# The end of routing in a hybrid block with a PEER feed-forward: six row products, the gathers' index tiles and the splits for the gates in another order

## The chip, the cores and the metric

One core of a Trainium2 chip runs the whole block. The metric is the time of one execution on the device in microseconds (us), the median of the runs. Engines are named as the profile names them: PE is TensorE (matmuls; PEld its weight loads), DVE is VectorE, ACT is ScalarE, POOL is GpSimd, SP issues most of the transfers. POOL also issues transfers of its own, and all of the gathers.

## The reference

A residual block on 512 tokens of width 1024, in float32: an RMS norm, a gated MLP group and a chunked attention group, an output projection, and then PEER, a feed-forward of 16384 single-neuron experts. The part that matters here is PEER:

```python
q = (xb @ w_query).reshape(PEER_TOKEN_BLOCK, PEER_HEADS, 2, PEER_HALF)
sc = jnp.einsum('thpd,hpkd->thpk', q, sub_keys).astype(jnp.float32)
s_top, i_top = lax.top_k(sc, PEER_TOPK)
...
best, pos = lax.top_k(cand, PEER_TOPK)
eidx = jnp.take_along_axis(cand_idx, pos, axis=-1)
g = jax.nn.softmax(best, axis=-1)
u = jnp.take(expert_u, eidx, axis=0)
h = jax.nn.gelu(jnp.einsum('thkd,td->thk', u, xb))
vv = jnp.take(expert_v, eidx, axis=0)
return jnp.einsum('thk,thkd->td', (g * h.astype(jnp.float32)).astype(xb.dtype), vv)
```

For each token and each of 8 heads, 16 experts are chosen (`eidx`) and weighted (`g`). The input row is multiplied with each chosen row of `expert_u`, and the results weight the rows of `expert_v`.

## The kernel before, in words

Two ways of computing PEER share the tokens. For most tokens the kernel multiplies densely: each of the 128 tiles of `expert_u` (512 KB each, `in_uT`) is loaded, split into a high and a low half (`hi` on ACT, L154; `lo` on DVE or POOL, L155) and multiplied on PE with the tokens' input in three products per step (`mm3`, L192 to L194, 8 steps a tile, 24 matmuls); an activation (L716) empties the result's PSUM bank, of which there are two, into `act`. The chosen weights are spread into a dense gate matrix, and a second product with the tiles of `expert_v` (L1168) ends the kernel. For the first 128 tokens, and for the last 64 (`UX`), the kernel gathers the chosen rows instead: an indirect transfer issued by POOL fetches one row of `expert_u` for each of 128 partitions (128 x 1024 float32), and DVE multiplies it with the input rows and sums it up (the "row product").

The last 64 tokens have 8 x 16 choices each, and two choices stand side by side on the 128 partitions, so there are 64 such gathers, 8 per head. They are the ones that the change touches:

- `indices_early(h)` brings one head's indices into `eui`: half of them by a small transfer on POOL's queue (L668), half by a cast on POOL (L669).
- `gather_early(n, ...)` issues the next n gathers (L653) into one of 6 row buffers (`ROWA`).
- `dots_early(lag)` multiplies gathered rows until only `lag` are left (L662, on DVE), into `du`.

The stages around them are these. Routing goes over the heads; in it PE interleaves query products with tiles of `expert_u`. Behind the last head come eight tiles of `expert_u` (`BRIDGE`) on PE, while DVE chooses that head's experts (L732 to L792), the softmax runs (L798 to L803), and the indices are taken apart into digits (`indices_of`, L866 to L871, into `ff`). Then two held tiles (`HELD`) are split on POOL, and routing ends. In routing a scheduler sets the order, by priorities and by marks (`tc.issue_after`).

The gate stage is a loop of 48 iterations (n) and two more, written out by hand for PE, DVE, ACT and POOL. PE turns `ff` (`gates_of`, L941), DVE makes digits from it (`hb`, `lb`, L952 and L955), POOL multiplies these to `bm` (L963), DVE makes `am` (L971), PE multiplies the two two iterations later (L979, 16 to an iteration), ACT copies the result out (L982, `gst`), and every second iteration stores 1 MB. Between these PE works on a few steps of the tiles of `expert_u`, which POOL or DVE split. `own` is 40; at n = `own` - 7 = 33 the row products of the last 64 tokens must be finished.

```python
if n < own - 7 and n % 3 < 2:
    gather_early(1, gat, ROWA)
dots_early(LAGE)
```

Of the kernel before, what the change touches and what calls it, by code (L numbers as in the profile page):

```python
# [11 lines left out]
I32 = mybir.dt.int32  # L12
# [7 lines left out]
P = 128  # L20
D = 1024
S = 512
TT = S // P
# [3 lines left out]
NH = 8  # L27
TOPK = 16
# [15 lines left out]
UX = 64  # L44
# [4 lines left out]
HS = NH * TOPK // 2  # L49
HK = TOPK // 2  # L50
# [9 lines left out]
ROWA = 6  # L60
LAGE = 3
BRIDGE = 8
EARLY = 6
# [29 lines left out]
def hybrid_block(tc, x, ln1, w_in, gng, wsT, bsb, qkg, bias, w_out, ln2, wq, skT, uT, ud, vd, out):  # L93
    nc = tc.nc
    ctx = ExitStack()
    with ctx:
# [10 lines left out]
        def pa():  # L107
            return ps_a.tile([P, 512], F32, name="pa", tag="pa")
# [13 lines left out]
        loads, splits, ready = [], [], []  # L122
        roots, behind_scale, behind_norm = [], [], []

        def queued_behind(marks):

            ctx = ExitStack()
            for i in marks:
                ctx.enter_context(tc.issue_after(i))
            return ctx  # L130
# [495 lines left out]
        eidx = rt.tile([P, TT, NH * TOPK], F32, name="eidx")  # L626
# [8 lines left out]
        gat = gat_ctx.enter_context(tc.tile_pool(name="gat", bufs=1, side="right"))  # L635
# [5 lines left out]
            nc.sync.dma_start(row[i * UX:(i + 1) * UX, :], xbd[1, P - UX:, :])  # L641
        nc.scalar.copy(xbu[:, 0:512], row[:, 0:512])
        nc.scalar.copy(xbu[:, 512:], row[:, 512:])
        eui = gat.tile([P, HS], I32, name="eui")
        du = gat.tile([P, HS], F32, name="du")
        dots = gat.tile([P, NH, 2, HK], F32, name="dots")
        early, issued = [], []

        def gather_early(n, rows_of, n_rows):

            for j in early[:n]:
                row = rows_of.tile([P, D], F32, name="rowe", tag="rowe", bufs=n_rows)
                nc.gpsimd.indirect_dma_start(out=row, out_offset=None, in_=ud,  # L653
                                             in_offset=bass.IndirectOffsetOnAxis(ap=eui[:, j:j + 1], axis=0))
                issued.append((j, row))
            del early[:n]

        def dots_early(lag):

            while len(issued) > lag:  # L660
                j, row = issued.pop(0)
                nc.vector.scalar_tensor_tensor(row, row, 1.0, xbu, op0=ALU.mult, op1=ALU.mult,  # L662
                                               accum_out=du[:, j:j + 1])

        def indices_early(h):

            js = slice(h * HK, (h + 1) * HK)
            nc.gpsimd.dma_start(eui[0:P - UX, js], eidx[P - UX:P, TT - 1, h * TOPK + HK:(h + 1) * TOPK])  # L668
            nc.gpsimd.tensor_copy(eui[P - UX:P, js], eidx[P - UX:P, TT - 1, h * TOPK:h * TOPK + HK])  # L669

        def ready_early(h):
            early.extend(range(h * HK, (h + 1) * HK))
# [38 lines left out]
        def multiply_tile(whole=False):  # L711
            multiply_some(KT, whole)
# [169 lines left out]
        for h in range(NH + 1):  # L882
            if h < NH:
                candidates(h)
            with queued_behind(found):
                dots_early(0)
            if h == NH:
                for i, _ in enumerate(first_products(sum(FILL) + BC, BRIDGE, nc.gpsimd, True)):
                    behind.append(done[0])
            if h > 1:  # L890
                with tc.issue_after(splits[0]):
                    indices_early(h - 2)
                    ready_early(h - 2)
                    gather_early(EARLY, gat, ROWA)
            if h > 0:
                hs = slice((h - 1) * TOPK, h * TOPK)
                ps = pa()
                mask = ps[:, 0:6 * ND * TOPK].bitcast(U32)
                powers = ps[:, 8 * ND * TOPK:8 * ND * TOPK + 6].bitcast(U32)
                nc.vector.tensor_copy(powers, bits)  # L900
                tree = rq.tile([P, ND, TOPK, 32], F32, name="tree", tag="tree", bufs=1)
                with tc.issue_after(behind[BRIDGE // 2 - 2]) if behind else ExitStack():
                    cand = pairs(rq, *top_pos.pop(h - 1)[:2], ND, ps[:, 6 * ND * TOPK:8 * ND * TOPK], True)
                with tc.issue_after(behind[BRIDGE // 2 - 1]) if behind else ExitStack():
                    choose(rq, cand, ND, gate[:, GT:, hs], eidx[:, GT:, hs], mask, tree,
                           nc.vector.tensor_copy if h >= NH - 1 else nc.scalar.copy, powers)
            if h == 4:

                with queued_behind(splits):
                    nc.gpsimd.tensor_copy(xch, xbh[:, :, T0:T0 + NDU])  # L910
                    nc.gpsimd.tensor_copy(xcl, xbl[:, :, T0:T0 + NDU])
# [10 lines left out]

        for _ in range(HELD):
            split_next()
        indices_early(NH - 1)
        ready_early(NH - 1)
        dots_early(0)
        routing.close()
        xn_ctx.close()

# [77 lines left out]
        engines = {getattr(mybir.EngineType, e) for e in ("PE", "DVE", "Activation", "Pool")}  # L1008
        own = steps - UX // TC
        with tc.manual_schedule(engines=engines):  # L1010
            gather_early(1, gat, ROWA)
            multiply_tile()
            gs[0] = gates_of(GT, ff.pop(0))
            dgs = {0: digits(gs[0], 0)}
# [2 lines left out]
            for n in range(steps + LEAD):  # L1017
# [11 lines left out]
                    activate_tile()  # L1029
                if n < steps:  # L1030
                    ams[n] = first_one_hot(gs[t], c)
                if n < own - 7 and n % 3 < 2:
                    gather_early(1, gat, ROWA)
                dots_early(LAGE)
                if t + 1 < ND:
                    if c == per - 5:
                        ff[t + 1] = indices_of(GT + t + 1)
# [210 lines left out]
```

## Time and profile before

| | |
|---|---|
| Median of three runs | 1442.33 us (1438.95 to 1442.57) |
| The profiled execution | 1436.48 us, of which 1434.4 us span |
| Granted TensorE clock, mean | 0.993 |
| End of routing, the last bridge tile to the first bm | 417 to 442 us |
| Gate stage | 442 to 592 us |
| Second product | 606 us to the end |

The span goes from the first to the last instruction. Starts in the trace are counted from its beginning. A row of the trace gives the start, the length, the engine, the line, the operation, what it writes and reads, and in brackets how long the engine stood idle before it and what it waited for. PE's matmuls are pipelined, so that a row's length is longer than the distance to the next row.

### The profile page before, as it was taken

Reading aid. Unit: us, or ns where it says so; the run is one execution under the profiler, and the core shown is the slowest. Engines: PE = TensorE matmul, PEld = TensorE weight load, DVE = VectorE, ACT = ScalarE, POOL = GpSimd, SP = SyncE. Lnnn points to the kernel's source line nnn. Section 1 sums busy time; section 2 is a strip of 40 time slices with the busy share of each in tenths; the row PEclk is TensorE's granted clock in tenths of the full one; section 3 lists DMA queues with packets and bytes.
Section 4 is the critical chain, followed back from the end, with each engine's and each line's share of the span. In section 5 each row is a group of like instructions: output and inputs, shape, how many; then the busy total and the mean of one; then the engine's idle time right before and its main releaser. Section 6 shows DMA issues by size and latency. Waiting matters only on the chain.

```text
span 1434.4 us, 21711 instructions
## 1 busy us (share of the span) xinstructions
PE 1391.9 (97%) x7838; PEld 1229.5 (86%) x7838; DVE 1150.5 (80%) x2502; ACT 611.4 (43%) x957; POOL 700.6 (49%) x487
## 2 busy tenths in 40 slices
PE   9999999999987978999999999999999999999998
PEld 7887788898986978898988898998998998888887
DVE  5537755998996888599999999889879888688883
ACT  5447635434442434554543444343333333333331
POOL 0002104678769988424554646545546455254520
PEclk9999999999998999999999999999999999999999
DMA  4352225667667998988998999999999989689981
GB/s 168 126 191 74 89 104 191 206 229 276 216 225 248 300 313 251 294 296 310 332 351 312 339 349 368 347 389 356 376 339 359 361 326 378 243 326 353 340 332 70
DMA packets 164330, 396.24 MB, mean 276 GB/s; under 512 B 12880, under 2 KB 75232, under 8 KB 162176
## 3 DMA queue, kind: packets, MB, share of 16 engines
q1 hardware_dynamic: 64640, 194.14, 37.6%
q0 software_dynamic: 48176, 173.46, 32.9%
q10 hardware_dynamic: 51408, 27.27, 6.6%
q8 instruction: 61, 1.00, 0.3%
q14 instruction: 45, 0.37, 0.1%
HBM read 363.34 MB, written 31.46 MB: 275 GB/s over the span
## 4 chain that ended last, share of the span: by engine, by line
PE 76%; DVE 9%; POOL 5%; DMA 4%; issue 3%; ACT 2%; another core or an unknown queue 0%; ACTq 0%; POOLq 0%; DVEq 0%; SPq 0%
PE pa L1168 22%; PE px L1168 11%; PE pu L194 9%; PE pu L192 9%; PE pu L193 9%; PE pa L192 4%; PE pa L979 3%; PE pa L193 3%; PE pa L194 3%; POOL bm L963 2%; POOL rowe L653 1%; DMA gd<-gst 1%; DVE lo L155 1%; POOL lo L155 1%; DVE row L1109 1%
## 5 line engine op out<-in xcount | busy, mean ns | idle before, releaser
L154 ACT ACTIVATE hi<-raw 128x1024 fp32r<-128x1024 f32 x296 | 312.8, 1058 | 468.5 <-DMA raw<-in_vd 124.0
L155 DVE TENSOR_TENSOR lo<-raw,hi 128x1024 fp32r<-128x1024 f32 x241 | 295.8, 1229 | 78.3 <-ACT hi L154 76.0
L1107 POOL DMA_INDIRECT row<-in_ud,eint x128 | 199.0, 1555 | 193.6 <-DVE acc L1120 129.8
L1118 POOL DMA_INDIRECT row<-in_vd,eint x128 | 180.6, 1411 | 165.3 <-DVE row L1109 110.9
L194 PE MATMUL pu<-xch,lo 128*128 128x320 f32 x784 | 244.7, 312 | 8.1 <-POOL lo L155 4.9
L192 PE MATMUL pu<-xch,hi 128*128 128x320 f32 x784 | 248.9, 317 | 2.0 <-ACT act L716 2.0
L193 PE MATMUL pu<-xcl,hi 128*128 128x320 f32 x784 | 244.2, 311 | 0.0
L1168 PE MATMUL pa<-lo,wh 128*128 128x512 f32 x512 | 199.7, 390 | 0.0
L1168 PE MATMUL pa<-hi,wh 128*128 128x512 f32 x512 | 199.3, 389 | 0.0
L155 POOL TENSOR_TENSOR lo<-raw,hi 128x1024 fp32r<-128x1024 f32 x55 | 131.4, 2403 | 98.3 <-ACT hi L154 95.7
L1120 DVE SCALAR_TENSOR_TENSOR acc<-row,hw,acc 128x1024 f32<-128x1024 f32 x128 | 164.9, 1288 | 2.0 <-DMA row<-in_vd,eint 1.9
L1109 DVE SCALAR_TENSOR_TENSOR row<-row,xb 128x1024 f32<-128x1024 f32 x128 | 157.8, 1235 | 1.7 <-DMA row<-in_ud,eint 1.7
L1168 PE MATMUL pa<-hi,wl 128*128 128x512 f32 x512 | 158.4, 389 | 0.0
L194 PEld LDWEIGHTS pu<-xch,lo 128*128 128x128 f32 x784 | 149.2, 190 | 8.9 <-POOL lo L155 5.4
L192 PEld LDWEIGHTS pu<-xch,hi 128*128 128x128 f32 x784 | 149.5, 191 | 4.1 <-ACT act L716 2.5
L193 PEld LDWEIGHTS pu<-xcl,hi 128*128 128x128 f32 x784 | 149.5, 191 | 1.7
L979 PE MATMUL pa<-bm,am 128*128 128x128 f32 x768 | 97.3, 280 | 19.0 <-POOL bm L963 12.9
L1168 PEld LDWEIGHTS pa<-hi,wh 128*128 128x128 f32 x512 | 96.1, 188 | 20.6
L1168 PEld LDWEIGHTS pa<-lo,wh 128*128 128x128 f32 x512 | 96.1, 188 | 20.3
L1168 PEld LDWEIGHTS pa<-hi,wl 128*128 128x128 f32 x512 | 96.1, 188 | 20.2
L979 PEld LDWEIGHTS pa<-bm,am 128*128 128x128 f32 x768 | 92.2, 194 | 23.7 <-POOL bm L963 17.2
L1168 PE MATMUL px<-hi,wh 128*128 128x512 f32 x256 | 100.5, 393 | 3.3 <-ACT hi L154 3.3
(236 smaller groups left out, 2629.4 us busy)
## 6 DMA issues: line engine op xcount, KB each, us to landing
raw<-in_uT SPq DMA_DIRECT2D x128, 512.0 KB
raw<-in_vd SPq DMA_DIRECT2D x128, 512.0 KB
gd<-gst ACTq DMA_DIRECT2D x24, 1024.0 KB
gc<-gd SPq DMA_DIRECT2D x15, 1280.0 KB
raw<-in_w_in SPq DMA_DIRECT2D x19, 512.0 KB
raw<-in_wq SPq DMA_DIRECT2D x16, 512.0 KB
raw<-in_w_out SPq DMA_DIRECT2D x8, 512.0 KB
gc<-gd SPq DMA_DIRECT2D x15, 256.0 KB
```

The costliest lines, as they stand in the source:

```text
L154: nc.scalar.activation(hi, raw, AF.Copy)
L155: ins = eng.tensor_tensor(lo, raw, hi.bitcast(F32), op=ALU.subtract)
L192: nc.tensor.matmul(ps, lh[0], rh[0], start=first, stop=False)
L193: nc.tensor.matmul(ps, lh[0], rh[1], start=False, stop=False)
L194: nc.tensor.matmul(ps, lh[1], rh[0], start=False, stop=last)
L963: nc.gpsimd.tensor_tensor(bm.rearrange("p t (h l) -> p t h l", l=BL), d[0][:, ts_, :, None].to_broadcast(full), d[1][:, ts_, None, :].to_b ...
L979: nc.tensor.matmul(ps[:, i * P:(i + 1) * P], am[:, 4 * q + i, :], bm[:, 4 * q + i, :], start=True, stop=True)
L1107: nc.gpsimd.indirect_dma_start(out=row, out_offset=None, in_=ud, in_offset=bass.IndirectOffsetOnAxis(ap=eint[:, j:j + 1], axis=0))
L1109: nc.vector.scalar_tensor_tensor(row, row, 1.0, xb0, op0=ALU.mult, op1=ALU.mult, accum_out=hw[:, j:j + 1])
L1118: nc.gpsimd.indirect_dma_start(out=row, out_offset=None, in_=vd, in_offset=bass.IndirectOffsetOnAxis(ap=eint[:, j:j + 1], axis=0))
L1120: nc.vector.scalar_tensor_tensor(acc0, row, hw[:, j:j + 1], acc0, op0=ALU.mult, op1=ALU.add)
L1168: nc.tensor.matmul(accs[t][half], (wh, wh, wl)[k][:, b, tok], w[b][k % 2][:, ds_], start=first and k == 0, stop=last and k == 2)
```

## The change

- The indices of each head get a tile of their own (`eui[h]`), in place of one tile for all.
- In routing, head 6's index pair, its six gathers and head 7's index pair are no longer issued at their old places. The six gathers (the next six in the list, which are rows of heads 4 and 5) come behind the splits of the two held tiles.
- The row products of these six gathers are no longer made in routing. In the gate loop each iteration from n = 1 makes at most one row product.
- The index pairs of heads 6 and 7 move into iterations 1 and 2 of the gate loop. The loop's gathers start at n = 2 and come in three of four iterations; the one gather ahead of the loop goes.

```diff
-        eui = gat.tile([P, HS], I32, name="eui")
+        eui = [gat.tile([P, HK], I32, name=f"eui{h}") for h in range(NH)]
...
-        def dots_early(lag):
+        def dots_early(lag, most=NH * HK):
 
-            while len(issued) > lag:
+            while len(issued) > lag and most > 0:
+                most -= 1
...
-            if h > 1:
+            if 1 < h < NH:
                 with tc.issue_after(splits[0]):
                     indices_early(h - 2)
                     ready_early(h - 2)
                     gather_early(EARLY, gat, ROWA)
...
         for _ in range(HELD):
             split_next()
-        indices_early(NH - 1)
-        ready_early(NH - 1)
-        dots_early(0)
+        with tc.issue_after(splits[0]):
+            gather_early(EARLY, gat, ROWA)
...
         with tc.manual_schedule(engines=engines):
-            gather_early(1, gat, ROWA)
             multiply_tile()
...
-                if n < own - 7 and n % 3 < 2:
+                if n in (1, 2):
+                    indices_early(NH - 3 + n)
+                    ready_early(NH - 3 + n)
+                if n:
+                    dots_early(LAGE, 1)
+                if 1 < n < own - 7 and n % 4 != 1:
                     gather_early(1, gat, ROWA)
-                dots_early(LAGE)
```

PE, ACT and SP keep their order; POOL and DVE change theirs. On POOL, from the bridge's last four splits (L155) to the loop's first bm, there stand in a row before:

```order
L155 TENSOR_TENSOR lo<-raw,hi 128x1024 x4
L653 DMA rowe<-in_ud,eui 128x1024 x3
L668 DMA eui<-eidx 64x8
L669 CAST eui<-eidx 64x8
L653 DMA rowe<-in_ud,eui 128x1024 x3
L155 TENSOR_TENSOR lo<-raw,hi 128x1024 x2
L653 DMA rowe<-in_ud,eui 128x1024
L155 TENSOR_TENSOR lo<-raw,hi 128x1024
L668 DMA eui<-eidx 64x8
L669 CAST eui<-eidx 64x8
L963 TENSOR_TENSOR bm<-hb,lb 128x1024
```

and now, from the same place to just behind the loop's third bm (eui_2081 to eui_2084 are the tiles of heads 4 to 7):

```order
L155 TENSOR_TENSOR lo<-raw,hi 128x1024 x6
L653 DMA rowe<-in_ud,eui_2081 128x1024 x4
L653 DMA rowe<-in_ud,eui_2082 128x1024 x2
L155 TENSOR_TENSOR lo<-raw,hi 128x1024
L962 TENSOR_TENSOR bm<-hb,lb 128x1024 x2
L668 DMA eui_2083<-eidx 64x8
L669 CAST eui_2083<-eidx 64x8
L962 TENSOR_TENSOR bm<-hb,lb 128x1024
L668 DMA eui_2084<-eidx 64x8
L669 CAST eui_2084<-eidx 64x8
L653 DMA rowe<-in_ud,eui_2082 128x1024
L155 TENSOR_TENSOR lo<-raw,hi 128x1024
```

The two held splits have moved ahead of all gathers, and both index pairs behind the first bm's. On the same piece of POOL the order also names what each instruction waits for; DMASW0 to DMASW7 are the eight semaphores that POOL's own transfers use in turn:

```order
L653 DMA rowe<-in_ud,eui_2081 128x1024 [waits DMASW5_49,DVE_49]
L653 DMA rowe<-in_ud,eui_2081 128x1024 [waits DMASW6_49,DVE_49]
L653 DMA rowe<-in_ud,eui_2081 128x1024 [waits DMASW7_49,DVE_49]
L653 DMA rowe<-in_ud,eui_2082 128x1024 [waits DMASW0_49,DVE_49]
L653 DMA rowe<-in_ud,eui_2082 128x1024 [waits DMASW1_49,DVE_49]
L155 TENSOR_TENSOR lo<-raw,hi 128x1024 [waits DMAHW6_49,PE_49,Activation_49]
L962 TENSOR_TENSOR bm<-hb,lb 128x1024 [waits DVE_49,DMAHW0_49,PE_49,Activation_49]
L962 TENSOR_TENSOR bm<-hb,lb 128x1024
L668 DMA eui_2083<-eidx 64x8 [waits DMASW2_49]
L669 CAST eui_2083<-eidx 64x8 [waits DMASW4_49,DMASW5_49,DMASW3_49,DMASW6_49,DMASW1_49,DMASW7_49,DMASW0_49,Pool_49]
```

The cast of head 6 lists seven of the eight, among them those of the six gathers ahead of it, though these read the tiles of heads 4 and 5. On DVE, in the choice of the last head's experts, there stand before:

```order
L662 SCALAR_TENSOR_TENSOR rowe,du<-rowe,px 128x1024
L736 MAX_INDEX bpos<-gate,rep_4500 128x8
L798 TENSOR_TENSOR ex<-gate 128x384
L781 TENSOR_TENSOR pa<-bpos,pa 128x288
L662 SCALAR_TENSOR_TENSOR rowe,du<-rowe,px 128x1024
L790 COPY_PREDICATED tree<-pa,cand 128x48x18
L801 TENSOR_REDUCE zs<-ex 128x24
L790 COPY_PREDICATED tree<-pa,tree 128x48x16
```

and now, at the same place:

```order
L736 MAX_INDEX bpos<-gate,rep_4493 128x8
L798 TENSOR_TENSOR ex<-gate 128x384
L781 TENSOR_TENSOR pa<-bpos,pa 128x288
L790 COPY_PREDICATED tree<-pa,cand 128x48x18
L790 COPY_PREDICATED tree<-pa,tree 128x48x16
L801 TENSOR_REDUCE zs<-ex 128x24
```

The six row products that stood in this piece and behind it now stand one by one behind the `am` of iterations 1 to 6 of the gate loop.

More of the change, by code (lines that the diff above doesn't have):

```diff
@@ L653, in gather_early @@
                 nc.gpsimd.indirect_dma_start(out=row, out_offset=None, in_=ud,
-                                             in_offset=bass.IndirectOffsetOnAxis(ap=eui[:, j:j + 1], axis=0))
+                                             in_offset=bass.IndirectOffsetOnAxis(ap=eui[j // HK][:, j % HK:j % HK + 1], axis=0))
                 issued.append((j, row))
             del early[:n]
-        def dots_early(lag):
-            while len(issued) > lag:
+        def dots_early(lag, most=NH * HK):
+            while len(issued) > lag and most > 0:
+                most -= 1
                 j, row = issued.pop(0)
@@ L665, in indices_early @@
         def indices_early(h):
-            js = slice(h * HK, (h + 1) * HK)
-            nc.gpsimd.dma_start(eui[0:P - UX, js], eidx[P - UX:P, TT - 1, h * TOPK + HK:(h + 1) * TOPK])
-            nc.gpsimd.tensor_copy(eui[P - UX:P, js], eidx[P - UX:P, TT - 1, h * TOPK:h * TOPK + HK])
+            nc.gpsimd.dma_start(eui[h][0:P - UX, :], eidx[P - UX:P, TT - 1, h * TOPK + HK:(h + 1) * TOPK])
+            nc.gpsimd.tensor_copy(eui[h][P - UX:P, :], eidx[P - UX:P, TT - 1, h * TOPK:h * TOPK + HK])
         def ready_early(h):
```

## The prediction

> **What bounds the kernel now.** I read the page's busy shares first, then the stretches around the change, then who TensorE waited for.
>
> ```profile
> span 1434.4 us, 21711 instructions
> PE 1391.9 (97%) x7838; PEld 1229.5 (86%) x7838; DVE 1150.5 (80%) x2502; ACT 611.4 (43%) x957; POOL 700.6 (49%) x487
> ```
>
> TensorE is the bound: only 42.5 us of the span are not matmul. The stretches say where they lie (columns: stretch, its length, busy us of PE, PEld, DVE, ACT, POOL, granted clock, DMA share, GB/s):
>
> ```profile
> 417.00:442.33 25.33, 18.38 (x112) 17.62 (x111) 22.62 (x71) 7.06 (x10) 15.78 (x15) 0.87 0.65 223
> 442.33:470.00 27.67, 21.65 (x154) 20.35 (x154) 16.76 (x28) 10.66 (x17) 26.77 (x16) 0.94 0.72 219
> 470.00:510.00 40.00, 37.44 (x298) 35.92 (x297) 35.83 (x59) 17.24 (x30) 37.99 (x24) 1.00 1.03 325
> 510.00:553.00 43.00, 33.96 (x268) 32.22 (x269) 34.57 (x56) 18.78 (x33) 35.92 (x21) 1.00 0.94 294
> 606.00:1434.00 828.00, 821.27 (x4307) 728.52 (x4305) 710.15 (x1203) 325.17 (x466) 389.47 (x264) 1.00 0.88 328
> ```
>
> The first is the end of routing, the next three the gate stage's early part, the last the second product, where TensorE is busy 821.27 of 828: what is won before 606 stays won. The change lies in the first row, with 6.95 us of idle TensorE and a granted clock of 0.87. Its waits there and shortly behind (engine, line, releaser, total, times, longest):
>
> ```profile
> PE pa L979 <- POOL bm L963: 6.0, 3, 2.5
> PE pu L194 <- POOL lo L155: 4.9, 1, 4.9
> PE pu L192 <- ACT act L716: 2.0, 1, 2.0
> ```
>
> TensorE in order of time (start, length, instruction, idle before):
>
> ```profile
> 426.01 0.31 PE L192 MATMUL pu<-xbh,hi 128*128 128x320 f32 x1
> 426.30 0.31 PE L194 MATMUL pu<-xbh,lo 128*128 128x320 f32 x1
> 428.62 0.41 PE L192 MATMUL pu<-xch,hi 128*128 128x320 f32 x1 [2.02 <-ACT act L716]
> 434.06 0.64 PE L194 MATMUL pu<-xch,lo 128*128 128x320 f32 x1 [4.88 <-POOL lo L155]
> 437.69 0.42 PE L192 MATMUL pu<-xch,hi 128*128 128x320 f32 x1
> ```
>
> 426.30 is the last matmul of the bridge, whose steps are 0.145 us (426.01 to 426.30 is two). The next tile starts late and slow: from 434.06 to 437.69 its 13 steps take 0.28 each. Why the split was late is on POOL:
>
> ```profile
> 414.88 2.42 POOL L155 TENSOR_TENSOR lo<-raw,hi 128x1024 fp32r<-128x1024 f32 x1 [1.89 <-ACT hi L154]
> 417.44 0.96 POOL L653 DMA_INDIRECT rowe<-in_ud,eui  x1
> 419.95 0.94 POOL L653 DMA_INDIRECT rowe<-in_ud,eui  x1 [0.30 <-issue]
> 420.90 0.59 POOL L668 DMA_DIRECT2D eui<-eidx  x1
> 427.18 0.19 POOL L669 CAST eui<-eidx 64x8 int32<-64x8 f32 x1 [5.69 <-DMA rowe<-in_ud,eui]
> 431.42 4.91 POOL L155 TENSOR_TENSOR lo<-raw,hi 128x1024 fp32r<-128x1024 f32 x2
> 437.47 2.39 POOL L155 TENSOR_TENSOR lo<-raw,hi 128x1024 fp32r<-128x1024 f32 x1
> 442.07 0.19 POOL L669 CAST eui<-eidx 64x8 int32<-64x8 f32 x1 [1.69 <-DMA rowe<-in_ud,eui]
> 442.33 1.94 POOL L963 TENSOR_TENSOR bm<-hb,lb 128x1024 f32<-128x1024 f32 x1
> ```
>
> Both splits at 431.42 stand behind three gathers, a cast that waits 5.69 us for gathered rows to land, and three gathers more; bm 0 stands behind a second such cast.
>
> **Part 1, splits ahead of gathers.** Their hi halves are ready early:
>
> ```profile
> 417.39 1.06 ACT L154 ACTIVATE hi<-raw 128x1024 fp32r<-128x1024 f32 x1 [1.26 <-POOL lo L155]
> 426.30 0.52 ACT L799 ACTIVATE ex<-ex 128x384 f32<-128x384 f32 x1 [2.73 <-DVE ex L798]
> 426.84 1.28 ACT L716 ACT_TABLE_LOAD   x1
> 428.13 0.77 ACT L716 ACTIVATE act<-pu 128x320 f32<-128x320 f32 x2
> ```
>
> The one at 417.39 is the second tile's. So the splits run 417.4 to 419.8 and 419.8 to 422.2, far ahead of 426.6: the 4.88 us go. What is late next is the activation that frees the product's bank: it waits for the softmax's exp, and that for VectorE.
>
> **Part 2, six row products out of the routing.** Their first and last, and the end of VectorE's chain (ff feeds the gate transposes, which feed hb and lb, the digits that bm needs):
>
> ```profile
> 422.95 1.22 DVE L662 SCALAR_TENSOR_TENSOR rowe<-rowe,px 128x1024 f32<-128x1024 f32 x1
> 425.73 0.54 DVE L798 TENSOR_TENSOR ex<-gate 128x384 f32<-128x384 f32 x1
> 435.88 1.27 DVE L662 SCALAR_TENSOR_TENSOR rowe<-rowe,px 128x1024 f32<-128x1024 f32 x1
> 438.68 0.56 DVE L871 CAST ff<-pa 128x384 f32<-128x384 int32 x1
> 440.59 0.41 DVE L952 TENSOR_TENSOR lb<-iota_k,pa 128x256 f32<-128x256 f32 x1
> ```
>
> Two of them (2.3 us) and a gap of 0.2 stand ahead of ex, so ex ends near 423.8, exp near 424.3, its table change near 425.6, and the activations reach the bank by 426.6: the 2.02 us go. All six are 6 x 1.15 = 6.9 us of pitch and some 2 us of gaps and waits for rows, so ff ends near 430.2 and not 439.24. lb, which came 1.8 behind ff, is there at about 431.9. TensorE: tile 426.6 to 430.1 (24 steps of 0.145), the transposes at once, the second tile to 434. Its gain is 2.02 + 4.88 + 13 x (0.28 - 0.145) = 8.6 us.
>
> **Part 3, POOL to the gate loop.** Six gathers 422.2 to 429.8 (pitch 1.25), the third split to 432.2, lb there by then, bm 0 at 432.2 (10.1 sooner), bm 1 to 436.1. Then the new place of head 6's index pair, behind bm 1: 0.59 for its DMA, and a cast. The tile per head does not by itself free that cast: in the order it still lists the semaphores of the six gathers, so it waits until the sixth row, issued at 428.5, has landed. How long a row takes is in the chain:
>
> ```profile
> 399.88 7.42 DMA rowe<-in_ud,eui
> 419.95 7.08 DMA rowe<-in_ud,eui
> ```
>
> 7.1 us gives 435.6, before the cast is reached at 436.7: nothing. By bytes: six rows of 0.524 MB and three weight tiles of the same size beside them are 4.72 MB; 223 GB/s at a share of 0.65 means 343 with full queues, so 13.8 us from 422.2, which is 436.0. That is one end; the other is under (d). Behind the cast stands bm 2, which would end at 439.2 and is wanted by TensorE at 441.6, so the first 2.4 us of a wait are free. I take 0.4 on POOL. Head 7's pair follows bm 2 (0.9), with no such wait left. One gather ahead of bm 0, those behind bm 0 and bm 1, and the index pair ahead of bm 0 leave this place, which pays for it. With gather and split between, bm 3 ends at 445.5, bm 4 at 451.0, bm 5 at 456.4.
>
> ```profile
> 454.81 2.05 PE L979 MATMUL pa<-bm,am 128*128 128x128 f32 x16 [1.03 <-POOL bm L963]
> 460.24 2.05 PE L979 MATMUL pa<-bm,am 128*128 128x128 f32 x16 [2.50 <-POOL bm L963]
> ```
>
> These are products 3 and 4: 9.2 sooner by POOL, with the same waits ahead of them, since gather and split still stand between these bm's. The lead of the loop is the smaller of the two, 8.6.
>
> **Part 4, the loop.** Its 22 gathers are the same number as before (one of them stood ahead of it) and the last again falls in iteration 30, but two fewer are out when product 4 comes. POOL pays these two back behind it, 1.1 each (0.96 and the gap): the 9.2 become 7.0 by iteration 30, below TensorE's 8.6, if POOL sets the pace all the way. It is busy 37.99 of 40 from 470 to 510 but only 35.92 of 43 behind that, so of this 1.6 I take 0.6. VectorE has six products more, 7.3 us. Nine of the first ten iterations now hold one (five before), where POOL's splits leave VectorE idle: it is busy 16.76 of 27.67 from 442 to 470, which covers five; behind that it is busy 35.83 of 40 and takes the sixth. Between 0 and 2; I take 0.3. The transfers: two gathers (1.05 MB) more where the DMA share is 1.03. At 325 GB/s that is 3.2 us if the queue sets the pace there, and 0 if not; TensorE is busy 37.44 of 40, so near 0: I take 0.3. Nothing here is a saving.
>
> One rule speaks against part 1: the splits now run beside VectorE's copy of the last head's tree.
>
> ```profile
> 394.81 1.74 DVE L774 COPY tree<-cand 128x1536 f32<-128x1536 f32 x1
> 395.23 2.41 POOL L155 TENSOR_TENSOR lo<-raw,hi 128x1024 fp32r<-128x1024 f32 x1 [1.73 <-ACT hi L154]
> 419.06 1.74 DVE L774 COPY tree<-cand 128x1536 f32<-128x1536 f32 x1
> ```
>
> Such a copy with a split on top of it (394.81) takes as long as one without (419.06), and the split its usual 2.4. So I take nothing. The Trainium skill ("SBUF — State Buffer", Who interferes with whom) holds that a VectorE copy may take the port pair it shares with GpSimd, and that the later of the two blocks fully. By that rule the sum below would be 4.2, as in (b); these rows do not bear it out.
>
> **Sum.** 8.6 - 0.6 - 0.3 - 0.3 = 7.4 us. The profiled execution took 1436.48 with 1434.4 of span, so 1429.1. The median of the three runs is 1442.33, 5.85 above that execution; taken from the median, 1434.9.
>
> **Rivals.** (a) The transfers set the pace of iterations 7 to 30: for it speaks the share of 1.03, against it TensorE's 37.44 of 40 beside it. It keeps 8.6 - 0.6 - 0.3 - 3.2 = 4.5: 1437.8. (b) The copy is blocked by the splits: it starts at 422.2 and not 419.06, ff comes 3.2 later and TensorE waits for it behind its first tile: 7.4 - 3.2 = 4.2, 1438.1. (c) VectorE becomes the bound and pays all six products: 8.6 - 7.3 = 1.3, 1441.0; its idle time in 442 to 470 speaks against it. (d) Slower: the cast behind bm 1 holds POOL for the landing of six rows. If a row's 7.1 us grows with what is in flight, twice it puts the sixth at 442.7: 6.0 late, 2.4 free, 3.6 lost, 1438.5; three times, for six rows and three weight tiles together, puts it at 449.8: 13.1 late, 10.7 lost, the sum 3.3 us slower, 1445.6. It decides from a landing at 446.5, 18 us after issue; against it, rows took 7.1 to 7.4 with two or five others on their way. (e) The change does not do what it says, because the splits are held by something other than the gathers: the 4.88 and the slow clock stay and 2 us are won, 1440.3; the hi at 417.39 speaks against.
>
> **Chances.** Forecast 0.63, (a) 0.11, (b) 0.04, (c) 0.09, (d) 0.04 for its milder end and 0.06 for its slower one, (e) 0.03. A difference of 0.3%, 4.3 us, is what this kernel's measurement can tell from none. The forecast lies well beyond it, (a) and (b) about on it; of these two I count 0.10 as faster and 0.05 as same. (c), (e) and the mild (d) are same: faster 0.73, same 0.21, slower 0.06. The range goes from 1429.5 (8.6 won is 1433.7, and the lowest run lies 3.4 under the median; most of both) to 1441.0, which takes in all but the slow (d).
>
> **What would show it.** Right: the two splits of the held tiles directly behind the bridge's last, no wait of TensorE on lo or act between the bridge and the gate transposes, clock 1.0 there, first bm about 10 us sooner, the first gate product about 9 sooner, and its distance to the second product's start unchanged at about 160 us. Wrong: a wait of some us on the cast of head 6 with TensorE's products 2 and 3 late behind it; am named as releaser of gate products; longer waits of the gate copies on their stores; VectorE's tree copy longer than 1.74.

## The result, and the profile after

The change made the kernel about 8 to 9.5 us faster. Each row is one comparison on one chip, the two kernels run in turn:

| Kernel | Median, us | Kernel before, us | Ratio | 95% interval |
|---|---|---|---|---|
| changed kernel | 1432.05 (6 runs) | 1440.21 (6) | 0.9947 | 0.9928 to 0.9967 |
| changed kernel, second time | 1431.65 (11) | 1440.93 (31) | 0.9942 | 0.9923 to 0.9961 |
| changed kernel, third time | 1430.84 (8) | 1440.36 (25) | 0.9934 | 0.9908 to 0.9960 |
| kernel before against itself | 1440.43 (12) | 1440.02 (29) | 1.0007 | 0.9991 to 1.0023 |

The ratios are worked out from the single runs and are not the quotients of the medians. All three intervals leave out a difference under 0.3%. The runs of one kernel in one comparison scatter over 4 to 15 us. The first profiled execution after took 1434.77 us with a span of 1432.8; that of before, 1436.48, was below all its timed runs in the first comparison. One profile against one profile would have shown 1.7 us.

The busy shares, and the same stretches as before:

```profile
span 1432.8 us, 21711 instructions
PE 1394.0 (97%) x7838; PEld 1231.7 (86%) x7838; DVE 1155.3 (81%) x2502; ACT 611.7 (43%) x957; POOL 702.5 (49%) x487
```

```profile
417.00:442.33 25.33, 24.97 (x180) 24.74 (x179) 24.02 (x74) 10.92 (x16) 21.97 (x18) 1.00 0.59 211
442.33:470.00 27.67, 21.04 (x155) 19.98 (x153) 17.53 (x30) 11.53 (x19) 26.80 (x16) 0.94 0.92 284
470.00:510.00 40.00, 35.87 (x272) 34.71 (x272) 33.36 (x57) 16.82 (x30) 36.17 (x24) 0.96 1.04 336
510.00:553.00 43.00, 34.36 (x279) 33.26 (x278) 41.27 (x61) 18.20 (x32) 35.05 (x22) 0.99 0.98 297
```

In the first stretch TensorE is now busy 24.97 of 25.33 us (18.38 before) at a granted clock of 1.00 (0.87 before). The stretches behind it hold later work than before, since the loop begins some 9 us sooner. TensorE through that place in order of time:

```profile
426.89 0.31 PE L194 MATMUL pu<-xbh,lo 128*128 128x320 f32 x1
427.04 0.31 PE L192 MATMUL pu<-xch,hi 128*128 128x320 f32 x1
430.41 0.30 PE L194 MATMUL pu<-xch,lo 128*128 128x320 f32 x1
431.08 0.52 PE L940 MATMUL pa<-ident,ff 128*128 128x128 f32 x3 [0.36 <-PE pu L194]
431.43 0.27 PE L941 MATMUL pa<-ident,gate 128*128 128x128 f32 x1
...
446.02 2.05 PE L978 MATMUL pa<-bm,am 128*128 128x128 f32 x16 [1.02 <-POOL bm L962]
```

The bridge's last matmul at 426.89 is followed at once by the held tile, 24 steps of 0.147 us, and that by the gate transposes. The waits of 2.02 on act and 4.88 on lo are gone. The first wait on a bm is at 446.02, for bm 3. The first gate product starts at 436.83, 8.3 us sooner than the 445.09 of before. On GpSimd (POOL), which carries the moved order:

```profile
414.55 7.19 POOL L155 TENSOR_TENSOR lo<-raw,hi 128x1024 fp32r<-128x1024 f32 x3 [0.74 <-ACT hi L154]
421.88 0.96 POOL L653 DMA_INDIRECT rowe<-in_ud,eui  x1
...
428.44 0.94 POOL L653 DMA_INDIRECT rowe<-in_ud,eui  x1 [0.30 <-issue]
429.40 2.40 POOL L155 TENSOR_TENSOR lo<-raw,hi 128x1024 fp32r<-128x1024 f32 x1
432.97 3.84 POOL L962 TENSOR_TENSOR bm<-hb,lb 128x1024 f32<-128x1024 f32 x2 [1.18 <-DVE lb L951]
436.75 0.58 POOL L668 DMA_DIRECT2D eui<-eidx  x1
437.38 0.19 POOL L669 CAST eui<-eidx 64x8 int32<-64x8 f32 x1
437.65 1.93 POOL L962 TENSOR_TENSOR bm<-hb,lb 128x1024 f32<-128x1024 f32 x1
```

Three splits stand in a row up to 421.74, then six gathers, a split, and two bm's; the cast of head 6 at 437.38 has no wait beside it. And on VectorE (DVE), the last tree copy, ex, ff and lb:

```profile
418.74 1.75 DVE L774 COPY tree<-cand 128x1536 f32<-128x1536 f32 x1
423.01 0.54 DVE L798 TENSOR_TENSOR ex<-gate 128x384 f32<-128x384 f32 x1
430.42 0.56 DVE L871 CAST ff<-pa 128x384 f32<-128x384 int32 x1
432.33 0.41 DVE L951 TENSOR_TENSOR lb<-iota_k,pa 128x256 f32<-128x256 f32 x1
```

Profiles of one kernel start this stage at different times (the last tree copy at 417.97 and 419.06 in two profiles of the kernel before, at 417.11 to 420.97 in three of the changed one). So the stages are best compared by distances inside one trace, in us:

| Profile | tree copy to end of bm 0 | bm 0 to first product of the second stage | from there to the end |
|---|---|---|---|
| before | 25.21 | 157.6 | 832.5 |
| before, second | 25.01 | 160.4 | 833.4 |
| after | 16.17 | 164.6 | 833.3 |
| after, second | 16.15 | 164.1 | 831.3 |
| after, third | 16.14 | 155.7 | 834.4 |

The first column is what the change does: 9.0 us, the same in every profile to 0.2. The second column is the gate loop, which swings by 9 us within one kernel. The third varies by 3 us, and the kernel before lies in the middle of that.

### The profile page after: what moved, and what is told of

Read it like the earlier page. It is cut to its first block, busy times and chain, and to the rows that moved or that the text cites. A ratio compares the mean times of both kernels' runs of the same rounds, so it can differ in the third digit from the quotient of the medians.

```text
span 1432.8 us, 21711 instructions
## 1 busy us (share of the span) xinstructions
PE 1394.0 (97%) x7838; PEld 1231.7 (86%) x7838; DVE 1155.3 (81%) x2502; ACT 611.7 (43%) x957; POOL 702.5 (49%) x487
## 4 chain that ended last, share of the span: by engine, by line
PE 71%; DVE 13%; DMA 8%; ACT 3%; issue 3%; POOL 2%; SPq 0%; another core or an unknown queue 0%; ACTq 0%; DVEq 0%; POOLq 0%
PE pa L1170 21%; PE px L1170 11%; PE pu L194 8%; PE pu L193 8%; PE pu L192 8%; DMA gd<-gst 3%; PE pa L192 3%; PE pa L194 3%; PE pa L193 3%; PE pa L978 2%; DVE rowe L663 2%; DVE lo L155 2%; DMA raw<-in_vd 2%; DVE row L1111 1%; POOL rowe L653 1%
## 5 line engine op out<-in xcount | busy, mean ns | idle before, releaser
L155 DVE TENSOR_TENSOR lo<-raw,hi 128x1024 fp32r<-128x1024 f32 x241 | 298.9, 1242 | 73.9 <-ACT hi L154 72.9
L1109 POOL DMA_INDIRECT row<-in_ud,eint x128 | 202.5, 1582 | 195.0 <-DVE acc L1122 129.3
L1120 POOL DMA_INDIRECT row<-in_vd,eint x128 | 179.8, 1404 | 162.6 <-DVE row L1111 106.6
L155 POOL TENSOR_TENSOR lo<-raw,hi 128x1024 fp32r<-128x1024 f32 x55 | 131.3, 2402 | 95.0 <-ACT hi L154 94.3
L1111 DVE SCALAR_TENSOR_TENSOR row<-row,xb 128x1024 f32<-128x1024 f32 x128 | 157.6, 1234 | 2.9 <-issue 1.4
```

The lines of the kernel that those rows point to most:

```text
L155: ins = eng.tensor_tensor(lo, raw, hi.bitcast(F32), op=ALU.subtract)
L1111: nc.vector.scalar_tensor_tensor(row, row, 1.0, xb0, op0=ALU.mult, op1=ALU.mult, accum_out=hw[:, j:j + 1])
L1120: nc.gpsimd.indirect_dma_start(out=row, out_offset=None, in_=vd, in_offset=bass.IndirectOffsetOnAxis(ap=eint[:, j:j + 1], axis=0))
```

## The experiments

**The two parts apart.** First the splits ahead of the gathers, with the six row products back in routing:

```diff
         for _ in range(HELD):
             split_next()
         with tc.issue_after(splits[0]):
             gather_early(EARLY, gat, ROWA)
+        dots_early(0)
         routing.close()
```

> The changed kernel with the six row products put back at the end of routing. Theory (the two parts win only together): both splits are early, so the wait of 4.88 us on lo goes from the first held tile, but ff waits for the rows of the late gathers (issued 422 to 429, 7 us each) and the six products, and ends near 438 to 440; TensorE does its second tile and then waits 4 to 8 us for the gate transposes. First bm near 441 to 443, gain 0 to 2 us: 0.998 to 1.000 of the kernel before. Rival (the splits alone carry the gain): ff is not later than 434, gain 5 us or more, 0.9965 or less.

Measured: 1440.68 us against 1440.93, ratio 1.0007 (0.9988 to 1.0027). TensorE, VectorE's last row product, and GpSimd's first bm in its trace:

```profile
436.79 1.20 DVE L663 SCALAR_TENSOR_TENSOR rowe<-rowe,px 128x1024 f32<-128x1024 f32 x1
438.58 0.56 DVE L871 CAST ff<-pa 128x384 f32<-128x384 int32 x1
439.24 0.88 PE L941 MATMUL pa<-ident,ff 128*128 128x128 f32 x3 [10.36 <-issue]
441.60 3.83 POOL L963 TENSOR_TENSOR bm<-hb,lb 128x1024 f32<-128x1024 f32 x2 [10.65 <-DVE lb L952]
```

The splits were early and the held tile ran early, and then TensorE stood 10.36 us (4 to 8 were expected) ahead of the transposes of ff: the row names no releaser, but ff ended at 439.14 and the transposes began at 439.24. GpSimd stood 10.65 for lb. The last row, issued at 427.61, was multiplied from 436.79. From the tree copy to the end of bm 0 it took 25.6 us. The gain was nothing, as expected.

Then the row products alone: the gathers, index pairs and splits in their old order, but for the one gather ahead of the loop, which stays away.

```diff
-            if 1 < h < NH:
+            if h > 1:
...
-        with tc.issue_after(splits[0]):
-            gather_early(EARLY, gat, ROWA)
+        indices_early(NH - 1)
+        ready_early(NH - 1)
...
-                if n in (1, 2):
-                    indices_early(NH - 3 + n)
-                    ready_early(NH - 3 + n)
```

> The changed kernel with the gathers, index pairs and splits back in their old order at the end of routing; only the six row products stay in the gate loop. Theory (the two parts win only together): ff is done near 430, but the splits still end near 431 to 436, behind the cast that waits 5.7 us for rows, so TensorE waits 4 to 5 us on lo, and bm 0 stands behind the second cast and begins near 441 as before; gain 0 to 2.5 us: 0.998 to 1.000. Rival (taking the products off VectorE carries the gain, and the splits only add to it): bm 0 5 us or more sooner than before, 0.9965 or less.

Measured: 1438.58 us against 1440.93, ratio 0.9985 (0.9959 to 1.0011). GpSimd, VectorE and TensorE:

```profile
427.07 0.19 POOL L669 CAST eui<-eidx 64x8 int32<-64x8 f32 x1 [5.21 <-DMA rowe<-in_ud,eui]
431.32 6.98 POOL L155 TENSOR_TENSOR lo<-raw,hi 128x1024 fp32r<-128x1024 f32 x3
431.00 0.56 DVE L871 CAST ff<-pa 128x384 f32<-128x384 int32 x1
433.71 0.64 PE L194 MATMUL pu<-xch,lo 128*128 128x320 f32 x1 [6.56 <-POOL lo L155]
438.73 0.49 PE L940 MATMUL pa<-ident,ff 128*128 128x128 f32 x3
```

ff was ready at 431.56, but TensorE, which works in order, stood at the held tile for 6.56 us and reached ff's transposes at 438.73. bm 0 ended 23.2 us behind the tree copy, 2.0 sooner than before. There the cast ahead of bm 0 waited 1.69 us for a gathered row; here, with the gather ahead of the loop away, it waits for none, so this 2.0 is not the products' alone. Alone the parts give -0.0007 and 0.0015 of the time, together 0.0058: some 7 of the 8.4 us come only when both are made. The interval of the second reaches to 0.0041, so this share rests as much on the traces: bm 0 comes 0.5 us later with the first part, 2.0 sooner with the second and 9.0 sooner with both.

**A tile per head.** All heads' indices in one tile again:

```diff
-        eui = [gat.tile([P, HK], I32, name=f"eui{h}") for h in range(NH)]
+        euia = gat.tile([P, HS], I32, name="eui"); eui = [euia[:, h * HK:(h + 1) * HK] for h in range(NH)]
```

> The changed kernel with the gathers' indices of all heads in one tile again. Theory (the tile per head buys nothing at this place): the index pair of head 6 behind bm 1 finds its rows landed, its cast waits under 0.5 us, bm 0 to bm 5 end at the same distances from the last tree copy to within 1 us, and the time is that of the changed kernel, 0.993 to 0.997 of the kernel before. Rival (it is the tile per head that frees the cast): the cast waits 3 us or more, bm 2 and what follows come so much later, 0.997 to 0.999.

Measured: 1434.15 us against 1440.02, ratio 0.9962 (0.9942 to 0.9981). The place in question on GpSimd:

```profile
431.93 3.84 POOL L962 TENSOR_TENSOR bm<-hb,lb 128x1024 f32<-128x1024 f32 x2 [1.22 <-DVE lb L951]
435.72 0.58 POOL L668 DMA_DIRECT2D eui<-eidx  x1
436.34 0.19 POOL L669 CAST eui<-eidx 64x8 int32<-64x8 f32 x1
436.61 1.93 POOL L962 TENSOR_TENSOR bm<-hb,lb 128x1024 f32<-128x1024 f32 x1
```

The cast waits for nothing here either, and bm 0 to bm 8 end at the same distances from the tree copy as in the changed kernel, to 0.1 us. So the tile does nothing at this place. The ratio lies 0.002 above that of the changed kernel, inside both intervals; whether a single tile costs a us or two earlier in routing, where it also gives another order, these runs can't tell.

**Who pays for the six row products.** They were cut to 32 of 1024 columns, so that VectorE had some 6.5 us less to do; the kernel leaves the other 992 columns out of these dots:

```diff
-                nc.vector.scalar_tensor_tensor(row, row, 1.0, xbu, op0=ALU.mult, op1=ALU.mult,
+                w = w_of[0] if most == 0 and short and short.pop() else D
+                nc.vector.scalar_tensor_tensor(row[:, 0:w], row[:, 0:w], 1.0, xbu[:, 0:w], op0=ALU.mult, op1=ALU.mult,
                                                accum_out=du[:, j:j + 1])
...
+        short, w_of = [1] * 6, [32]
```

> The changed kernel with the six row products that it moved into the gate loop done on 32 of the 1024 columns; their dots are wrong. It takes some 6.5 us of VectorE's work out of iterations 1 to 6. Theory (VectorE has that time free behind GpSimd's splits): the time stays within 1.5 us of the changed kernel, 0.993 to 0.996 of the kernel before, bm 0 to bm 8 keep their distances to within 0.3 us. Rival (VectorE pays for the six and its backlog is handed down to iterations 25 to 35, where it is busy 41 of 43 us): 3 us or more faster, 0.9925 or less.

Measured: 1434.55 us against 1440.36, ratio 0.9939 (0.9914 to 0.9964), where the changed kernel on the same chip had 0.9934. Its row for the loop's start:

```profile
442.33:470.00 27.67, 22.10 (x161) 20.96 (x159) 14.40 (x28) 12.12 (x20) 26.71 (x17) 0.94 0.91 285
```

VectorE is busy 14.40 us there (17.53 in the changed kernel), bm 0 to bm 8 take 30.0 us as with the whole products, and no gain is seen. VectorE had the time there. The interval takes in the rival's 0.9925; against it stands the trace, where the way from the tree copy to the second stage, 180.7 us, is as long as in the changed kernel's first profile.

**Who pays for the gathers.** The loop's 22 gathers were cut to half rows. The kernel leaves out the other half of each row, and the doubling of the index that half rows would need; it makes each row product in two halves, which is an estimated 3 to 4 us more for VectorE:

```diff
-                nc.gpsimd.indirect_dma_start(out=row, out_offset=None, in_=ud,
+                nc.gpsimd.indirect_dma_start(out=row[:, 0:w], out_offset=None, in_=ud.rearrange("e (a d) -> (e a) d", d=w),
...
+                if w < D:
+                    nc.vector.scalar_tensor_tensor(row[:, 0:w], row[:, D - w:], 1.0, xbu[:, D - w:], op0=ALU.mult,
+                                                   op1=ALU.mult, accum_out=du[:, j:j + 1])
...
-                    gather_early(1, gat, ROWA)
+                    gather_early(1, gat, ROWA, D // 2)
```

> The changed kernel with the gate loop's 22 gathers fetching half rows (0.26 MB each and not 0.52), and each row product done in two halves on VectorE, the second on what the first left; it computes wrong dots for these rows. 5.8 MB less to move in the loop, some 17 us of transfers at 330 GB/s, and 3 to 4 us more on VectorE. Theory (GpSimd and VectorE, not the transfers, set the loop's pace): within 2 us of the changed kernel, 0.993 to 0.997 of the kernel before, though the gate copies' waits on their stores shrink by half or more. Rival (the transfers set it: DMA share 1.04 from 470 to 510, and gate copies wait up to 5.7 us for their stores): 3 us or more faster than the changed kernel, 0.9925 or less.

Measured: 1433.86 us against 1440.02, ratio 0.9953 (0.9939 to 0.9968).

```profile
470.00:510.00 40.00, 37.03 (x287) 36.06 (x287) 37.76 (x81) 18.75 (x32) 38.29 (x25) 0.96 0.91 273
```

The DMA share falls from 1.04 to 0.91, and GpSimd stays busy 38.29 of 40 us: it issues the same instructions. The gate copies waited 13.3 us for their stores (34.4, 28.6 and 36.7 in the changed kernel's profiles), less than half, as expected. In its trace bm 0 to bm 29 took 94.4 us (97.8, 96.3 and 96.6 in the changed kernel's), so transfers may hold 2 or 3 us there; the time shows no gain, against a rival that wanted 3 us or more. That VectorE's added work hides a part of a gain is not excluded.

**Where the loop swings.** The kernels were profiled again:

> The kernel before a second time, for a second profile. Theory (the first profile of it was a lucky execution: 1436.5 us, where the median is near 1441): the end of routing is as it was (from the last tree copy to the end of bm 0 about 25.2 us, TensorE's 4.9 us wait on lo), and the gate loop from the end of bm 0 to the first product of the second stage, 157.6 us in the first profile, takes 160 to 164 here, with a VectorE split or the gate product held for several us beside bm's. Rival (the loop of the kernel before has no such hold-ups, and the change itself makes the loop 7 us longer): 157 to 159 us again. The ratio is 1.000 within 0.002 under both.

> The changed kernel a second time, with a profile of its own. Theory (the loss in the loop is chance): the end of routing comes out as in the first profile (no wait of TensorE on lo or act, first bm ending near 437), but the VectorE operations that took 5.39 us (lo at 530.27) and 5.21 us (gate at 554.64) there take other times here, since it depends on a few tenths of a us whether GpSimd's next bm is already running when they come; the lead over the profile of the kernel before at the last bm then lies between 2 and 9 us and not at 2.5 again. Rival (the loss is set by the order): both operations are long again, to within 0.5 us, and the lead falls from 8.7 to 2.5 at the same two places. The time: 0.993 to 0.997 of the kernel before under both.

> The changed kernel a third time, for a third profile. Theory: from the last tree copy to the end of bm 0 16.1 us as in the first two (25.2 and 25.0 before), the loop from there to the first product of the second stage 164 within 1.5 (157.6 and 160.4 before): the loop keeps back some 5 of the 9 us, so the timed gain of 8 to 9 us is only half explained by the traces. Rival (the loop's length is chance): it is 160 or less here. The time: 0.993 to 0.996 of the kernel before under both.

The kernel before: ratio 1.0007 (0.9991 to 1.0023), its loop 160.4 us, with a split of 4.50 us and a gate product of 7.63, as its theory had it. The changed kernel: ratios 0.9942 and 0.9934; loops of 164.1 and 155.7. In the second profile the last bm ends 1.9 us ahead of that in the first profile of before, just outside the 2 to 9 that were expected. The third profile decides against "the loop keeps 5 us": its loop is 1.9 us shorter than the shortest of the kernel before, and its last bm ends 12.9 us ahead of that in the first profile of before (11.0 when both are counted from the tree copy). Nor are the hold-ups at fixed places: the split that took 5.39 us in the first profile took 1.44 in the second and 1.22 in the third, while the gate product took 5.21, 7.05 and 1.90. (Such a split takes VectorE 1.22 us where nothing holds it.) First profile, the split and the gate product on VectorE, and what GpSimd and TensorE do around the product:

```profile
530.27 5.39 DVE L155 TENSOR_TENSOR lo<-raw,hi 128x1024 fp32r<-128x1024 f32 x1 [0.15 <-ACT hi L154]
554.64 5.21 DVE L683 TENSOR_TENSOR gate<-gate,dots 64x128 f32<-64x128 f32 x1 [2.47 <-ACT dots L682]
553.99 5.69 POOL L962 TENSOR_TENSOR bm<-hb,lb 128x1024 f32<-128x1024 f32 x3
562.12 5.71 POOL L962 TENSOR_TENSOR bm<-hb,lb 128x1024 f32<-128x1024 f32 x3 [2.43 <-DVE lb L951]
559.90 0.33 PE L941 MATMUL pa<-ident,gate 128*128 128x128 f32 x1 [1.53 <-DVE gate L683]
```

The product ends at 559.85, right behind the third bm (559.68). GpSimd then has no digits, since the lb that it needs stands behind the held product on VectorE: it waits 2.43 us. The second profiles of the changed kernel and of the kernel before, in which a split and three bm's went first:

```profile
552.44 7.05 DVE L683 TENSOR_TENSOR gate<-gate,dots 64x128 f32<-64x128 f32 x1 [0.64 <-ACT dots L682]
556.06 7.63 DVE L683 TENSOR_TENSOR gate<-gate,dots 64x128 f32<-64x128 f32 x1
```

The same place in the third profile:

```profile
546.94 1.90 DVE L683 TENSOR_TENSOR gate<-gate,dots 64x128 f32<-64x128 f32 x1 [2.38 <-ACT dots L682]
546.77 13.31 POOL L962 TENSOR_TENSOR bm<-hb,lb 128x1024 f32<-128x1024 f32 x7
```

Here it got in behind the first bm of seven, and nobody waited. To separate the operands from the rest, the gelu was written to PSUM:

```diff
-                nc.scalar.activation(dots[own], dots[own], AF.Gelu_apprx_tanh)
-                nc.vector.tensor_tensor(gate[own, TT - 1, :], gate[own, TT - 1, :],
-                                        dots[own].rearrange("p a b k -> p (a b k)"), op=ALU.mult)
+                dp = pa()[:, 0:NH * TOPK]
+                nc.scalar.activation(dp[own].rearrange("p (a b k) -> p a b k", a=NH, b=2), dots[own], AF.Gelu_apprx_tanh)
+                nc.vector.tensor_tensor(gate[own, TT - 1, :], gate[own, TT - 1, :], dp[own], op=ALU.mult)
```

> The changed kernel, with the gelu of the last 64 tokens' dots written to PSUM, so that the product gate times dots on VectorE (64x128) reads one operand from SBUF and one from PSUM, not two from SBUF. Theory (VectorE operations with two SBUF operands are held while GpSimd works, as the Trainium skill has it in SBUF - State Buffer, Who interferes with whom; no run here has separated it yet): that product takes below 0.5 us beside running bm's (5.21 in the changed kernel, 2.00 in the kernel before), TensorE's wait of 1.5 us for it and GpSimd's of 2.4 behind it go; 1 to 3 us sooner than the changed kernel, 0.992 to 0.995 of the kernel before. Rival (it is long for its own sake, by its 64 partitions or its wait for the gelu): 2 us or more here too, no gain.

```profile
549.06 2.39 POOL L155 TENSOR_TENSOR lo<-raw,hi 128x1024 fp32r<-128x1024 f32 x1
549.58 0.29 DVE L684 TENSOR_TENSOR gate<-gate,pa 64x128 f32<-64x128 f32 x1
551.37 9.48 POOL L962 TENSOR_TENSOR bm<-hb,lb 128x1024 f32<-128x1024 f32 x5
```

This product takes 0.29 us, in the two kernels below that have it too. That it runs at 549.58 beside GpSimd's split (549.06 to 551.45 in that trace) shows that it is the second SBUF operand that waits. TensorE's wait of 1.53 us for the product and GpSimd's of 2.43 behind it are gone. The way from the end of bm 34 to that of bm 47, in every profile:

| Gate product | Profiles | bm 34 to bm 47, us |
|---|---|---|
| held, 5.1 to 7.6 us | before second, after, after second, dots only, one tile, half rows, short products | 32.4, 32.4, 33.4, 32.4, 33.4, 32.4, 32.4 |
| not held, 0.3 to 2.0 us | before, after third, splits only, gelu in PSUM | 30.3, 29.6, 29.5, 30.4 |
| not held, 0.3 to 0.8 us, dots moved by SyncE (below) | dots by SyncE, both repairs, before with both | 32.1, 34.8, 34.1 |

By the first two rows a held product goes with 2 to 4 us more in a trace. Only the gelu in PSUM takes the hold away by an edit, so this is no clean price; the last row, where bm 34 comes without GpSimd's wait for the dots and the stretch is long without a hold, shows that other things stretch it as much. In time the hold can't be seen: 1432.41 us against 1440.93, ratio 0.9943 (0.9918 to 0.9967), where the changed kernel had 0.9942. The time lies in the theory's 0.992 to 0.995, but the 1 to 3 us against the changed kernel didn't come; whether the timed executions are rarely held, or the time is lost again, stays open.

**Repairs at the loop's end.** The dots' small transfer, for which GpSimd stands idle until the last rows are multiplied, was given to SyncE:

```diff
-                nc.gpsimd.dma_start(dots[own, :, 1, :], d[0:P - UX])
+                nc.sync.dma_start(dots[own, :, 1, :], d[0:P - UX])
```

> The changed kernel with the small transfer of the dots (L680) issued by SyncE and not by GpSimd. Before it GpSimd stands idle for 5.1 us in the first profile of the changed kernel (2.9 in the second, 3.6 in the kernel before) until VectorE has multiplied the last rows. Theory (GpSimd sets the pace there): with bm in its place the wait goes, TensorE's wait of 3.5 us on the next bm with it, and 1.5 to 3.5 us are won against the changed kernel: 0.991 to 0.994 of the kernel before. Rival (the rows of the last gathers set it, through the gate product): VectorE's am's and TensorE's products stand behind the same row products, and what GpSimd does sooner is waited for elsewhere: no gain, 0.994 to 0.996.

Measured: 1429.71 us against 1440.02, ratio 0.9936 (0.9919 to 0.9954). That is within the theory's span, but its interval reaches into the rival's, and the changed kernel itself had 0.9934 to 0.9947, so no gain is shown. In its trace the loop took 158.6 us. GpSimd's wait for the rows went, and one of 2.74 us came instead, for ScalarE's half of a split:

```profile
542.72 1.93 POOL L962 TENSOR_TENSOR bm<-hb,lb 128x1024 f32<-128x1024 f32 x1 [0.28 <-POOL bm L962]
547.39 2.37 POOL L155 TENSOR_TENSOR lo<-raw,hi 128x1024 fp32r<-128x1024 f32 x1 [2.74 <-ACT hi L154]
```

Both repairs together, in the changed kernel and in the kernel before:

> The changed kernel with both repairs of the loop's end: the dots' transfer issued by SyncE, and the last gelu in PSUM so that the gate product has one SBUF operand. Theory (the two hold GpSimd and VectorE up one after the other): gate product 0.3 us, no idle GpSimd before the dots' transfer, loop 157 to 160 us; 2 to 4 us faster than the changed kernel, 0.991 to 0.993 of the kernel before. Rival (each opens only room that the other, or the stores, close again): as SyncE's alone, 0.9935 to 0.995.

> The kernel before with the same two repairs, and nothing of the change. Theory (the repairs belong to the loop's end and the change to the end of routing, and they add): 1 to 3 us faster than the kernel before, 0.998 to 0.9993, and the change is worth as much on top of them as without, 7 to 9 us. Rival (the kernel before loses more there than the changed one, and the change gained part of its 8 us by that): 4 us or more, 0.997 or less, and the change is then worth 5 us or less on top.

Measured on one chip: 1430.26 against 1440.36, ratio 0.9929 (0.9904 to 0.9955), beside 0.9934 for the changed kernel there; and 1437.37, ratio 0.9973 (0.9954 to 0.9992). In the changed kernel the ratio lies in the theory's span, as do its loop (158.2 us) and its gate product (0.29), and what the repairs add can't be told from nothing; the kernel before gains 3 to 4 us by them, between what the theory (up to 3) and the rival (4 or more) had. The change on top of them is worth 0.9929/0.9973 = 0.9956, some 6 us. That is inconclusive: the two intervals taken together reach from about 2 to 11 us. The version with both is the quickest by its ratio, and not measurably quicker than the changed kernel.

## Why the prediction was right

It forecast 7.4 us and measured were 8.2, 9.3 and 9.5. The time, 1434.9, was 2.9 too high; 0.8 of that is the gain, and the rest that the median it was taken from, 1442.33, stood 2.1 above the 1440.21 of the longer comparison.

**Part 1, the splits.** Forecast done at 422.2, measured 421.74; no wait on lo, clock 1.00. Right. Read as a price of its own, 4.88 and 1.75 for this part is wrong: alone it was worth nothing, since ff then held TensorE for 10.36 us. The sum of 8.6 holds for the two parts together, and so does its size: bm 8 ends 8.2 to 8.5 us nearer to the tree copy.

**Part 2, the row products.** exp's end was forecast near 424.3 and measured at 424.12; ff at 430.2 against 430.98, lb at 431.9 against 432.74. These 0.8 us are the one miss at this place, and with a tree copy 0.3 earlier they are 1.1: GpSimd waited 1.18 us for lb where the prediction had lb there in time. bm 0 came 9.0 us sooner and not 10.1. TensorE did not wait for bm 0 to bm 2, but bm 3, for which it waits, came late with them: with the tree copy counted in, some 0.8 us later than forecast, which brings the 9.2 forecast for this place down to the 8.2 to 8.5 above. Read as a price of its own, 2.02 is too little for this part, since without it part 1 has no value.

**Part 3, GpSimd to the loop.** bm 3, 4 and 5 were forecast to end at 445.5, 451.0 and 456.4, and ended at 445.96, 451.41 and 456.81, with the same waits ahead of their products. The cast of head 6 waited for nothing, with a tile per head and with one tile; rival (d) had no ground.

**Part 4, the loop.** 0.6, 0.3 and 0.3 were charged. VectorE's and the transfers' terms of 0.3 can't be told from nothing: less work for either moved no time that could be measured, which speaks against (c) and (a) as well; (e) is excluded by the splits at 414.55. GpSimd's is of the right kind: bm 0 to bm 29 took 96.0 and 94.7 us before and 97.8, 96.3 and 96.6 after, 1.5 us more in the mean, with scatter as large.

**The signs.** The distance from the first gate product to the second stage was to stay at about 160 us: it was 156.8 and 158.7 before and 162.6, 162.1 and 153.8 after, so the loop's scatter hides whether it did. Two of the signs for being wrong showed, neither as a cost that can be put down to the change. am was named as releaser of gate products for 3.8 us in the first profile after, but for 2.9 in the second of before and for none in the third after. The gate copies waited 34.4, 28.6 and 36.7 us for their stores, against 31.1 and 28.4 before; TensorE's own waits for these copies were no longer (2.9, none and 2.1 us, against 5.9 and 1.7).

**The sums.** 2.02 + 4.88 + 13 x 0.135 is 8.66 and stands as 8.6. The range's lower end, 1429.5, is argued from 1433.7 and 3.4, but these give 1430.3. Neither moves the forecast.

**The rule on the copy.** The tree copy at 418.74 lies wholly beside GpSimd's splits (414.55 to 421.74) and took 1.75 us, as it does alone. So (b), by which it would have been blocked, did not happen. But that section of the Trainium skill ("SBUF — State Buffer", Who interferes with whom) also says that a VectorE instruction with two SBUF inputs contends with a GpSimd instruction that reads SBUF, and that, outside its two-port modes, one with at most one such input does not. This is borne out at places where the prediction did not look: VectorE operations with two SBUF operands took 5.39, 5.21, 7.05 and 7.63 us beside bm's and splits of GpSimd, and the product with one of them in PSUM 0.29. Part 4 has no term for it. It is no cost of the change, since the kernel before is held as well (7.63), and it is a part of the 9 us by which the loop of single traces swings. A reader of the first two profiles alone would have blamed the change for it.

**What stays open.** By the traces, tree copy to second stage is 184.1 us in the mean of two before and 177.6 in the mean of three after, 6.5 us; the timings say 8 to 9.5. With loops that swing by 9 us this is no contradiction, but the traces do not prove the last 1.5 to 3 us. bm 29 to bm 34 took 19.1 us in the first profile after and 14.3 in the third. The rows add up to this difference. GpSimd's wait ahead of the dots' transfer is 2.3 us longer (first profile, then third):

```profile
549.01 0.78 POOL L680 DMA_DIRECT2D dots<-du  x1 [5.11 <-DVE dots L679]
541.40 0.78 POOL L680 DMA_DIRECT2D dots<-du  x1 [2.82 <-DVE dots L679]
```

A wait for lb, which stands behind the held split on VectorE, is another 1.6, and a gather that took 1.79 us beside that split, and not 0.99, the last 0.8. What decides in an execution whether the split is held is not shown.

## What to carry to other kernels

Where an in-order engine waits for two late inputs one behind the other, price the pair: taking away one wait alone was worth 0 or 2 us here, both 8 to 9. Compare stages by distances inside one trace, and take a second profile of each kernel before a difference of a few us in a later stage is put down to the change. Ahead of a run of back-to-back GpSimd work, look for VectorE operations with two SBUF operands that others wait for, and give one operand a place in PSUM if it is free.

## What the runs showed of the hardware that was not expected

A VectorE operation with two SBUF operands can be held behind several GpSimd operations in a row, not just the one that runs when it comes: the gate product waited for three bm's (5.21 us), for a split and three (7.05 us), and in another execution got in behind the first of seven (1.90 us). A plain copy of 128 x 1536 beside splits (1.75 us), and VectorE operations that read one operand from PSUM beside bm's and splits (0.29 us; am's and row products at 1.2), were not held. GpSimd is slowed in turn: where a split ran on VectorE (574.87 to 576.10 in the first profile after), the two bm's that began at 575.17 took 4.61 us, where two took 3.84 at 432.97.
